# The first loop of a hybrid diffusion layer: shift rows on TensorE beside the scale rows, four row buffers ahead, and the context's x loaded last

## The chip, the cores and the metric

One NeuronCore of a Trainium2 chip runs the whole kernel. The metric is the device time of one execution in microseconds (us); lower is better. The kernel before was timed three times: 1124.28, 1126.04 and 1126.17 us, median 1126.04.

## What is computed

One layer over 512 latent tokens and 256 context tokens of width 1024: a half-step SwiGLU FFN, token mixing (latent attention beside a chunked gating MLP), and a second half-step FFN. Each sublayer first normalizes and modulates its input:

```python
def rms_norm(x, w):
    xf = x.astype(jnp.float32)
    y = xf * lax.rsqrt(jnp.mean(xf * xf, axis=-1, keepdims=True) + EPS)
    return (y * w.astype(jnp.float32)).astype(x.dtype)

def modulate(h, shift, scale):
    return h * (1 + scale) + shift

def ffn_sublayer(h_in, shift, scale, gate, norm_w, w1, w3, w2):
    h = modulate(rms_norm(h_in, norm_w), shift, scale)
    return h_in + 0.5 * gate * swiglu(h, w1, w3, w2)
...
    mx = jnp.split((jax.nn.silu(c) @ w_ada + b_ada)[:, None, :], N_MOD, axis=-1)
    mc = jnp.split((jax.nn.silu(c_ctx) @ w_ada + b_ada)[None, None, :], N_MOD, axis=-1)
...
    x = ffn_sublayer(x, mx[0], mx[1], mx[2], norm1_w, ffn1_w1, ffn1_w3, ffn1_w2)
    ctx = ffn_sublayer(ctx, mc[0], mc[1], mc[2], norm1_w, ffn1_w1, ffn1_w3, ffn1_w2)
```

`mx` and `mc` are the nine modulation vectors of the latent and of the context tokens. The first FFN needs two of them before anything else can be multiplied: the scale (`mx[1]`, `mc[1]`) and the shift (`mx[0]`, `mc[0]`), each a product of a 1024-vector with a 1024 x 1024 part of `w_ada`.

## The kernel before

All activations lie transposed: the 1024 features in eight slices `k` of 128 partitions, the tokens along the free axis, as two groups of 256 latent and 128 context tokens. Each fp32 matrix product is made of three fp32r products: an operand is split into a rounded high part and a remainder, and high x high, high x low and low x high are summed in PSUM.

The **first loop** goes over the eight slices of features. For slice `k` it makes the slice's shift and scale, makes the modulated activations of that slice, and multiplies them with the slice's part of the first four up-projection tiles (`NFIRST = 2` pairs). What one step consists of, with the names of the profile:

- loads on SyncE's queue (SP): `scale` (512 KB, the scale's columns of `w_ada` for this slice), `shift` (512 KB), and `raw` (256 KB of FFN weights). `x` comes first; the context's part of `x` comes in two loads of 128x8x128 (`load_x(..., slice(256, 384))`).
- the scale by TensorE: `ada_row` (L330 to 333) makes a row of four partial sums with eight matmuls of 32 weight columns, each in one of four 32-partition quarters of the bank `pa`; ScalarE copies it to `row`; `ada_col` (L340 to 342) turns it into a column pair (latent, context) with one matmul by `sel`; ScalarE makes `a` of it.
- the shift by VectorE: `ada_sum` calls `ada_dot` (L296), a multiply of the 128x1024 `shift` tile with `cb`, silu(c) spread over all partitions, that sums along the row into `accs` (the product itself goes to `junk`). There is one for the latent and one for the context vector of each slice, 16 in all. ScalarE adds the bias (`ada_s`, output `s`).
- `first_x` (VectorE) makes `hfull` = x * a * rstd; `first_h` (ScalarE) adds the shift and rounds to `hh`; `first_l` (VectorE) makes the remainder `hl`. `oph` (ScalarE) and `opl` (VectorE) split the weights.
- `first_half` and `first_mm` (L596, L604): the latent matmuls into `big`. `first_ctx` (L589): 12 matmuls for the context's part of one slice into two `mm` banks.
- once: the squares of `x`, their sum over features by a matmul with `ones` (L470, `sums`), the root `r` and the steps for `v` = rstd; for the context these are `square1`, `ctx_add`, and `sumc`, in the middle of the loop.

A list scheduler normally orders the program, but the first loop is under `nc.ordered = True`: VectorE, ScalarE and GpSimd keep the order in which the code is written, and so do the matmuls and the SP loads, which are wrapped in `pin`. These instructions all appear under line L59, the wrapper, so they are told apart by their tiles. A load waits until its buffer is free and until the load issued eight before it has landed, and all later loads wait behind it.

After the loop the first FFN goes on in the same manner, with weight tiles `raw` and `block` (from `wst`); its own modulation products (`ada_rest`) still use `cb` and `ada_dot`.

Of the kernel before, what the change touches and what calls it, by code (L numbers as in the profile page):

```python
# [17 lines left out]
P = 128  # L18
# [20 lines left out]
OPS = 5  # L39
# [134 lines left out]
def layer_kernel(ctx: ExitStack, tc: tile.TileContext, xT, wfirst, wst, wada, wuq, wkpe, cols, wrope, vnw, rope, out):  # L174
# [39 lines left out]
    accs = const.tile([P, NK, 2], F32, name="accs")  # L214
# [46 lines left out]
    sblk, units, raws_ = [], [], []  # L261

    def first_scale(k):
        ra = sp.tile([P, D], F32, tag="sa", bufs=3, name=f"scale_{k}")
        pin(nc.sync.dma_start(ra, wada[k][:, :D]))
        units.append([ra])

    def first_shift(k):
        if k % 2 == 0:
            pool, tag, bufs = (sp, "sb", 1) if k == 4 else (st.raw_pool, "block", BLOCKS)  # L270
            sblk.append(pool.tile([P, 2048], F32, tag=tag, bufs=bufs, name=f"shift_{k}"))
        rs_ = sblk[-1][:, (k % 2) * D : (k % 2) * D + D]
        pin(nc.sync.dma_start(rs_, wada[k][:, D:]))
        units[k].append(rs_)
# [6 lines left out]
    def first_units(k):  # L281
        first_scale(k)
        first_shift(k)
        first_raw(k)

    for k in range(3):
        first_units(k)
    nc.vector.tensor_reduce(sel, ident.rearrange("p (q c) -> p c q", c=32)[:, 0:2, :], axis=AX.X, op=ALU.add)
# [7 lines left out]
    def ada_dot(raw, c, which, to=None):  # L296
# [3 lines left out]
        nc.vector.scalar_tensor_tensor(  # L300
            out, raw, 1.0, cb[:, which, :], ALU.mult, ALU.mult,
            accum_out=acc[which][:, c : c + 1] if to is None else to,
        )
# [26 lines left out]
    def ada_row(d):  # L330
        for kt in range(NK):
            q = slice(kt % 4 * 32, kt % 4 * 32 + 32)
            pin(nc.tensor.matmul(pa[q, :P], scw[:, kt, :], units[d][0][:, kt * P : kt * P + P], start=kt < 4, stop=kt >= NK - 4))
# [6 lines left out]
    def ada_col(row, d):  # L340
        o = pcol[:, 2 * d : 2 * d + 2]
        pin(nc.tensor.matmul(o, row, sel, start=True, stop=True))
# [9 lines left out]
    def ada_shift(d, which):  # L352
        ada_sum(d, which)
        ada_s(d, which)
# [108 lines left out]
    def square1(j):  # L463
        sq = sp.tile([P, 512], F32, tag="sqx0", bufs=4, name=f"sq0_1{j}")
# [7 lines left out]
    def rstd_tiles(which):  # L472
        n = parts[which][1]
        return [sp.tile([P, n], F32, bufs=1, name=f"{s}{which}") for s in ("r0", "v")]
# [52 lines left out]
    put_cb(0)  # L527
    nc.vector.tensor_scalar_add(b1, col[:, COL_B : COL_B + 72], 1.0)
# [3 lines left out]
    def oph(k):  # L532
        ops[k] = st.pair() if k != OPS else [sp.tile([P, 512], F32R, tag="sqx0", bufs=4, name=f"op5{p}") for p in "hl"]
# [20 lines left out]
    put_cb(1)  # L554
    oph(0)
    steps(0)
    ada_row(0)
    row = ada_copy(0)
    late_sums(1)
    ada_col(row, 0)  # L560
    ada_sum(0, 0)
    ada_s(0, 0)
    root(1)
# [3 lines left out]
    first_units(3)  # L567
    ada_row(1)
    row = ada_copy(1)
    first_l(0, 0, 0)  # L570
    oph(1)
    steps(1)
    first_x(0, 0, 1)
    opl(1)
    first_h(0, 0, 1)
    first_units(4)
    load_x(0, 4, slice(256, 384))
# [35 lines left out]
    def step_open(k):  # L613
        ada_col(row, k + 1)
        if k + 2 < NK:
            ada_row(k + 2)

    sqs = []
    first_half(0)
    ada_col(row, 1)  # L620
    first_l(0, 0, 1)
    ada_row(2)
    row = ada_copy(2)
    ada_sum(1, 0)
    ada_s(1, 0)
    first_half(1)
    first_x(1, 0)
    first_h(1, 0)
    ada_sum(2, 0)
    first_l(1, 0)  # L630
    oph(2)
    opl(2)
    ada_s(2, 0)
    first_scale(5)
    load_x(4, 4, slice(256, 384))
    first_shift(5)
    first_raw(5)

    step_open(1)
    first_x(2, 0)  # L640
    first_h(2, 0)
    row = ada_copy(3)
    ada_sum(0, 1)
    first_l(2, 0)
    ada_sum(3, 0)
    oph(3)
    opl(3)
    ada_s(3, 0)
    ada_s(0, 1)
    step_mm(1)  # L650

    step_open(2)
    first_x(3, 0)
    first_h(3, 0)
    row = ada_copy(4)
    ada_sum(1, 1)
    oph(4)
    for j in (0, 1):
        sqs.append(square1(j))
    first_l(3, 0)  # L660
    ada_sum(4, 0)
    opl(4)
    ada_s(1, 1)
    ada_s(4, 0)
    step_mm(2)
    for k in (6, 7):
        first_scale(k)
        first_raw(k)
    for k in (6, 7):
        first_shift(k)  # L670

    step_open(3)
    first_x(4, 0)
    first_h(4, 0)
    for j in (2, 3):
        sqs.append(square1(j))
    row = ada_copy(5)
    ada_sum(5, 0)
    first_l(4, 0)
    ctx_add(2, 0)  # L680
    ctx_add(3, 1)
    ada_s(5, 0)
    oph(5)
    opl(5)
    ctx_add(2, 3)
    nc.vector.tensor_add(sqs[2][:, 0:256], sqs[2][:, 0:256], sqs[2][:, 256:512])
    step_mm(3)

    step_open(4)
    first_mm(4, 0)  # L690
    sumc = mm()
    sums(sumc, sqs[2][:, 0:256], True, True)
    first_mm(4, 1)
    first_x(5, 0)
    first_h(5, 0)
    row = ada_copy(6)
    first_l(5, 0)
    ada_sum(6, 0)
    ada_s(6, 0)
    rc = rstd_tiles(1)  # L700
# [4 lines left out]
    for j in (0, 1):  # L705
        first_x(j, 1)
        first_h(j, 1)
    ada_sum(2, 1)
    for j in (0, 1):
        first_l(j, 1)  # L710

    pcs += [mm() for _ in range(NFIRST)]
    step_open(5)
    first_x(6, 0)
    first_h(6, 0)
    row = ada_copy(7)
    ada_sum(3, 1)
    for j in (2, 3):
        ada_s(j, 1)
    first_l(6, 0)  # L720
    for j in (2, 3):
        first_x(j, 1)
        first_h(j, 1)
    ada_sum(7, 0)
    for j in (2, 3):
        first_l(j, 1)
    step_mm(5)
    for j in (0, 1):
        first_ctx(j)
    ada_s(7, 0)  # L730
    oph(6)
    opl(6)

    step_open(6)
    first_x(7, 0)
    first_h(7, 0)
    ada_sum(4, 1)
    first_l(7, 0)
    for j in (2, 3):
        first_ctx(j)  # L740
    oph(7)
    opl(7)
    ada_sum(5, 1)
    for j in (4, 5):
        ada_s(j, 1)
        first_x(j, 1)
        first_h(j, 1)
    ada_sum(6, 1)
    for j in (4, 5):
        first_l(j, 1)  # L750
    ada_sum(7, 1)
    for j in (6, 7):
        ada_s(j, 1)
        first_x(j, 1)
        first_h(j, 1)
    for j in (6, 7):
        first_l(j, 1)
    step_mm(6)

    step_mm(7)  # L760
    for j in range(4, NK):
# [1477 lines left out]
```

## Time and profile before

| | |
|---|---|
| median of three runs | 1126.04 us |
| the profiled execution | 1126.13 us |
| its span, first to last instruction | 1124.3 us |
| TensorE busy | 1109.6 us (99%) |
| VectorE busy | 906.1 us (81%) |
| ScalarE busy | 540.1 us (48%) |
| GpSimd busy | 311.4 us (28%) |
| first matmul after the first loop | at 66.94 us |

The span is counted from the first instruction; all positions below are us from there. The execution's own time is 1.8 us longer than its span. PE is TensorE, DVE VectorE, ACT ScalarE, SPq the queue of SyncE that issues loads. A row of the timeline reads: start, length, engine, line, operation, output <- inputs, number of instructions, and in brackets the idle time of the engine before it with what ended it. An fp32 matmul that isn't fp32r is recorded as two (x16 for eight). Lengths of neighbours on one engine overlap, so that the time an instruction takes in a stream is the distance between starts.

### The profile page before, as it was taken

The page shows a single profiled execution, that of the slowest core. Times are in us where ns is not written, and L with a number is a line of the kernel's source. Part 1 is how long each engine was busy: PE and PEld are TensorE (multiplying, and loading weights), DVE is VectorE, ACT ScalarE, POOL GpSimd, SP SyncE. Part 2 cuts the span into 40 slices and gives each one's busy share as a digit, 9 for nine tenths or more (in the row PEclk, how much of TensorE's full clock was granted, in tenths as well). Part 3 has the DMA queues.
Part 4 walks back from the last instruction along what each step waited for, and adds up shares of the span by engine and source line. Part 5 has one row for each costly group of instructions (what it writes and reads, how often), then busy time and mean ns, then how long its engine had stood idle before and what let it go on. Part 6 is the DMA issues. An engine that isn't in the chain of part 4 may idle for free.

```text
span 1124.3 us, 18769 instructions
## 1 busy us (share of the span) xinstructions
PE 1109.6 (99%) x7078; PEld 1060.7 (94%) x7078; DVE 906.1 (81%) x1669; ACT 540.1 (48%) x1119; POOL 311.4 (28%) x268
## 2 busy tenths in 40 slices
PE   8799999999999999999999999999999999999998
PEld 6699999999999999999998889999989989898997
DVE  7989999888888778866855899978886969686884
ACT  5555422441344213444755559985553535353451
POOL 0002402420343013300008427750014425162330
PEclk9999999999999999999999999999999999999999
DMA  9630253244234664322233211003221422233302
GB/s 350 215 113 20 102 194 121 96 164 151 94 131 150 230 207 167 129 66 87 85 131 93 76 38 35 25 20 116 73 95 57 148 79 84 105 113 113 114 1 94
DMA packets 35674, 125.89 MB, mean 112 GB/s; under 512 B 3712, under 2 KB 10624, under 8 KB 30976
## 3 DMA queue, kind: packets, MB, share of 16 engines
q1 hardware_dynamic: 35440, 124.63, 32.8%
q8 instruction: 56, 0.92, 0.3%
q14 instruction: 34, 0.28, 0.1%
q10 hardware_dynamic: 144, 0.06, 0.0%
HBM read 122.58 MB, written 2.10 MB: 111 GB/s over the span
## 4 chain that ended last, share of the span: by engine, by line
PE 91%; DVE 6%; ACT 1%; issue 1%; DMA 0%; POOL 0%; SPq 0%; DVEq 0%; POOLq 0%; ACTq 0%
PE mm L59 57%; PE one L59 20%; PE big L59 8%; PE mm L168 2%; PE mm L169 2%; PE mm L170 2%; DVE junk L59 1%; PE mm L589 1%; DVE opl L59 1%; DVE hfB L59 1%; DVE hfull L59 1%; DVE hl L59 1%; PE big L604 1%; DMA x<-xT 0%; DVE v L59 0%
## 5 line engine op out<-in xcount | busy, mean ns | idle before, releaser
L59 DVE TENSOR_TENSOR opl<-block,oph 128x512 fp32r<-128x512 f32 x216 | 192.3, 897 | 29.7 <-ACT oph L59 26.9
L59 POOL TENSOR_TENSOR block<-block 128x512 f32<-128x512 f32 x69 | 104.9, 1521 | 391.1 <-DVE opl L59 388.4
L59 ACT CAST oph<-block 128x512 fp32r<-128x512 f32 x216 | 133.8, 621 | 111.9 <-PE mm L59 85.1
L59 PE MATMUL mm<-gh,oph 128*128 128x384 f32 (+1 forms) x440 | 155.4, 353 | 0.0
L59 PE MATMUL mm<-gh,opl 128*128 128x384 f32 (+1 forms) x440 | 155.0, 352 | 0.0
L59 PE MATMUL mm<-gl,oph 128*128 128x384 f32 (+1 forms) x440 | 154.9, 352 | 0.0
L59 DVE SCALAR_TENSOR_TENSOR x<-mm,g,x 128x256 f32<-128x256 f32 (+2 forms) x184 | 84.6, 498 | 48.5 <-PE mm L59 48.2
L59 ACT CAST oph<-raw 128x512 fp32r<-128x512 f32 x115 | 69.9, 620 | 78.6 <-PE mm L59 53.1
L59 PEld LDWEIGHTS mm<-gh,opl 128*128 128x128 f32 x440 | 82.6, 188 | 5.7
L59 PEld LDWEIGHTS mm<-gl,oph 128*128 128x128 f32 x440 | 82.6, 188 | 5.6
L59 PEld LDWEIGHTS mm<-gh,oph 128*128 128x128 f32 x440 | 82.6, 188 | 5.6
L59 POOL TENSOR_TENSOR block<-s,block 128x512 f32<-128x512 f32 x35 | 48.0, 1371 | 143.7 <-DVE opl L59 143.1
L59 DVE TENSOR_TENSOR opl<-raw,oph 128x512 fp32r<-128x512 f32 x115 | 77.4, 688 | 7.2 <-ACT oph L59 6.5
L59 PE MATMUL mm<-hh,oph 128*128 128x384 f32 x192 | 64.9, 338 | 0.0
L59 PE MATMUL mm<-hh,opl 128*128 128x384 f32 x192 | 64.5, 336 | 0.0
L59 PE MATMUL mm<-hl,oph 128*128 128x384 f32 x192 | 64.5, 336 | 0.0
L59 DVE SCALAR_TENSOR_TENSOR junk<-raw,cb 128x1024 bf16<-128x1024 f32 x48 | 62.2, 1309 | 0.3 <-DMA raw<-wada 0.3
L59 POOL TENSOR_TENSOR s<-block 128x512 f32<-128x512 f32 x34 | 55.6, 1634 | 9.9 <-DMA block<-wst 9.9
L59 PE MATMUL one<-hh,opl 128*128 128x384 f32 x144 | 48.4, 336 | 0.0
L59 PE MATMUL one<-hh,oph 128*128 128x384 f32 x144 | 48.4, 336 | 0.0
L59 PE MATMUL one<-hl,oph 128*128 128x384 f32 x144 | 48.4, 336 | 0.0
L59 DVE SCALAR_TENSOR_TENSOR raw<-raw,cb 128x1024 f32<-128x1024 f32 x32 | 41.0, 1289 | 8.1 <-DMA raw<-wada 8.1
(685 smaller groups left out, 3403.0 us busy)
## 6 DMA issues: line engine op xcount, KB each, us to landing
raw<-wst SPq DMA_DIRECT2D x77, 512.0 KB, 3.9
block<-wst SPq DMA_DIRECT2D x36, 1024.0 KB, 4.9
raw<-wada SPq DMA_DIRECT2D x56, 512.0 KB, 4.3
scale<-wada SPq DMA_DIRECT2D x8, 512.0 KB, 8.4
shift<-wada SPq DMA_DIRECT2D x8, 512.0 KB, 8.9
x<-xT SPq DMA_DIRECT2D x5, 512.0 KB, 6.3
raw<-wfirst SPq DMA_DIRECT2D x8, 256.0 KB, 7.6
out<-x SPq DMA_DIRECT2D x7, 256.0 KB, 2.2
```

The lines of the kernel that those rows point to most:

```text
L59: return lambda *a, **k: self.tc.keep_in_program_order(f(*a, **k))
L168: nc.tensor.matmul(out, lh, rh, start=first, stop=False, skip_group_check=more)
L169: nc.tensor.matmul(out, lh, rl, start=False, stop=False, skip_group_check=more)
L170: nc.tensor.matmul(out, ll, rh, start=False, stop=last, skip_group_check=more)
L589: pin(nc.tensor.matmul(o, l[:, c], r, start=k == 0 and m == 0 and w == 0, stop=k == NK - 1 and m == 2, skip_group_check=True))
L604: pin(nc.tensor.matmul(two(pbs[i]), l[:, c], lat(r, k), start=False, stop=k == NK - 1 and m == 2, skip_group_check=True))
```

## The change

The shift is made like the scale. The shift's weights are laid out as the scale's are, and `ada_row` now makes 16 matmuls into the same bank: eight for the scale, with silu(c) in columns 0 and 1 of the 32 weight columns, and eight for the shift, with silu(c) in columns 2 and 3 (the tile `scw` is 34 wide, and the two halves are windows into it). `sel` has four columns, `ada_col` gives four, and ScalarE makes both `a` and `s` from them. The 16 `ada_dot` of the loop, `accs` and `ada_s` are gone.

```diff
-    scw = sp.tile([P, NK, 32], F32, bufs=1, name="sc")
-    sc = scw[:, :, 0:2]
-    sel = sp.tile([P, 2], F32, bufs=1, name="sel")
+    scw = sp.tile([P, NK, 34], F32, bufs=1, name="sc")
+    sc = scw[:, :, 2:4]
+    sel = sp.tile([P, 4], F32, bufs=1, name="sel")
...
+    def first_rows(k):
+        pool, tag, bufs = (sp, "sa", 2) if k % 2 else (st.raw_pool, "block", BLOCKS)
+        t = pool.tile([P, 2048], F32, tag=tag, bufs=bufs, name=f"scale_{k}")
+        units.append((t[:, :D], t[:, D:]))
+        for w in range(2):
+            pin(nc.sync.dma_start(units[k][w], wada[k][:, w * D : w * D + D]))
...
     def ada_row(d):
-        for kt in range(NK):
-            q = slice(kt % 4 * 32, kt % 4 * 32 + 32)
-            pin(nc.tensor.matmul(pa[q, :P], scw[:, kt, :], units[d][0][:, kt * P : kt * P + P], start=kt < 4, stop=kt >= NK - 4))
+        for w in range(2):
+            for kt in range(NK):
+                q = slice(kt % 4 * 32, kt % 4 * 32 + 32)
+                pin(nc.tensor.matmul(pa[q, :P], scw[:, kt, 2 - 2 * w : 34 - 2 * w], units[d][w][:, kt * P : kt * P + P],
+                                     start=w == 0 and kt < 4, stop=w == 1 and kt >= NK - 4))
...
     def ada_col(row, d):
-        o = pcol[:, 2 * d : 2 * d + 2]
+        o = pcol[:, 4 * d : 4 * d + 4]
         pin(nc.tensor.matmul(o, row, sel, start=True, stop=True))
         nc.scalar.activation(
-            pairs[0][1][:, d, :], o, AF.Identity, bias=b1n[:, d : d + 1], scale=col[:, COL_N1 + d : COL_N1 + d + 1])
-
-    def ada_sum(d, which):
-        ada_dot(units[d][1], d, which, accs[:, d, which : which + 1])
-
-    def ada_s(d, which):
-        nc.scalar.activation(mod_s[0][which][:, d : d + 1], accs[:, d, which : which + 1], AF.Identity, bias=col[:, d : d + 1])
+            pairs[0][1][:, d, :], o[:, 0:2], AF.Identity, bias=b1n[:, d : d + 1], scale=col[:, COL_N1 + d : COL_N1 + d + 1])
+        nc.scalar.activation(pairs[0][0][:, d, :], o[:, 2:4], AF.Identity, bias=col[:, d : d + 1])
...
-    first = np.concatenate([t[:, :, 1].transpose(2, 1, 0, 3).reshape(NK, P, 1024), t[:, :, 0].transpose(2, 3, 0, 1).reshape(NK, P, 1024)], 2)
+    first = np.concatenate([t[:, :, 1].transpose(2, 1, 0, 3).reshape(NK, P, 1024), t[:, :, 0].transpose(2, 1, 0, 3).reshape(NK, P, 1024)], 2)
```

Everything else in the loop is written in another order. The loads of four slices are issued at once instead of three, the context's `x` is loaded after seven of the eight `raw` tiles, its squares come in step 5 instead of steps 2 and 3 and its sum in step 6 instead of step 4, and all eight `first_ctx` come after the last latent matmul. `put_cb(1)`, ScalarE's copy of the context's `cb`, moves ahead of the first root. The loop's later part now reads:

```python
    for k in range(2, 5):
        step_open(k)
        next_h(k + 1)
        row = ada_copy(k + 2)
        first_l(k + 1, 0)
        oph(k + 2)
        opl(k + 2)
        if k == 2:
            first_raw(7)
        step_mm(k)
```

VectorE in the middle of the loop, before. A row is line, operation, output <- inputs and shape; `junk` is the output of a shift product, the number after a tile's name (`shift_0`) the slice where it has one:

```order
L59 TENSOR_TENSOR opl_373_374<-raw_252_253,oph_371_372 128x512
L59 SCALAR_TENSOR_TENSOR hfull_114<-x_71,a0_79,v0_214 128x2x256
L59 SCALAR_TENSOR_TENSOR junk_405_406,accs_87<-shift_0_129,cb_107 128x1024
L59 SCALAR_TENSOR_TENSOR hl_103<-hfull_114,s0_78,hh_102 128x2x256
L59 SCALAR_TENSOR_TENSOR junk_418_419,accs_87<-shift_4_279,cb_107 128x1024
L59 TENSOR_TENSOR opl_410_411<-raw_281_282,oph_408_409 128x512
```

The same place now, and on to the squares of the context's `x`:

```order
L59 TENSOR_TENSOR op6l_521<-raw_406_407,op6h_520 128x512
L59 SCALAR_TENSOR_TENSOR hfull_113<-x_71,a0_79,v0_215 128x2x256
L59 SCALAR_TENSOR_TENSOR hl_102<-hfull_113,s0_78,hh_101 128x2x256
L59 TENSOR_TENSOR op7l_561<-raw_441_442,op7h_560 128x512
L59 TENSOR_TENSOR sq0_11_566<-sq0_11_566,sq0_10_564 128x512
L59 TENSOR_TENSOR sq0_12_568<-sq0_12_568,sq0_11_566 128x512
L59 TENSOR_TENSOR sq0_13_570<-sq0_13_570,sq0_12_568 128x512
L59 TENSOR_TENSOR sq0_13_570<-sq0_13_570 128x256
L59 SCALAR_TENSOR_TENSOR hfull_113<-x_71,a0_79,v0_215 128x2x256
```

The two products between the modulations of neighbouring slices are gone; the adds of the squares now stand behind the split of the last weight tile and ahead of slice 7's `hfull`.

SyncE's loads from slice 4 on, before (`scale_4` is slice 4's; 128x8x128 is the context's `x`, and the last rows' `raw` and `block` from `wst` are weights for after the loop):

```order
L265 DMA scale_4_277<-wada 128x1024
L273 DMA shift_4_279<-wada 128x1024
L278 DMA raw_281_282<-wfirst 128x512
L258 DMA x_71<-xT 128x8x128
L265 DMA scale_5_343<-wada 128x1024
L258 DMA x_71<-xT 128x8x128
L273 DMA shift_4_279<-wada 128x1024
L278 DMA raw_347_348<-wfirst 128x512
L265 DMA scale_6_436<-wada 128x1024
L278 DMA raw_438_439<-wfirst 128x512
L265 DMA scale_7_441<-wada 128x1024
L278 DMA raw_443_444<-wfirst 128x512
```

And now (one `scale` tile holds scale and shift, so x2 is both):

```order
L267 DMA scale_4_276<-wada 128x1024 x2
L267 DMA scale_5_279<-wada 128x1024 x2
L271 DMA raw_346_347<-wfirst 128x512
L267 DMA scale_6_349<-wada 128x1024 x2
L271 DMA raw_358_359<-wfirst 128x512
L267 DMA scale_7_396<-wada 128x1024 x2
L271 DMA raw_406_407<-wfirst 128x512
L257 DMA x_71<-xT 128x8x128 x2
L127 DMA block_785_786<-wst 128x2048
L271 DMA raw_441_442<-wfirst 128x512
```

The context's loads moved behind slice 6's `raw`; the last `raw`, slice 7's, now stands behind both of them and behind a 1024 KB `block`.

TensorE at a step of the loop, before and then now (`row` is the copy that `ada_col` reads, `mm_157_158` the bank of the rows):

```order
L342 MATMUL mm_159_160<-sel_119,row_5_465 128x2
L333 MATMUL mm_157_158<-scale_6_436,sc_118 32x128 x8
L604 MATMUL big_285_286<-hh_102,oph_408_409 128x512 x2
L604 MATMUL big_285_286<-hh_102,opl_410_411 128x512 x2
L604 MATMUL big_285_286<-hl_103,oph_408_409 128x512 x2
```

```order
L334 MATMUL mm_159_160<-sel_118,row_5_477 128x4
L324 MATMUL mm_157_158<-scale_6_349,sc_117 32x128 x16
L581 MATMUL big_282_283<-hh_101,oph_435_436 128x512 x2
L581 MATMUL big_282_283<-hh_101,opl_437_438 128x512 x2
L581 MATMUL big_282_283<-hl_102,oph_435_436 128x512 x2
```

The row takes 16 matmuls instead of eight. Behind the loop each engine has the same instructions in the same order as before.

More of the change, by code (lines that the diff above doesn't have):

```diff
@@ L279, in first_raw @@
         raws_.append(rw[:, :W1])
[L281 to L288, printed above, removed]
+    for k in range(4):
+        first_rows(k)
+        if k < 3:
+            first_raw(k)
+    nc.vector.tensor_reduce(sel, ident.rearrange("p (q c) -> p c q", c=32)[:, 0:4, :], axis=AX.X, op=ALU.add)
     warm = mm()
@@ L294, in layer_kernel, with ada_dot @@
     nc.scalar.activation(epsc2, sc[:, 0, 0:1], AF.Abs_reciprocal_sqrt, bias=epsc, scale=0.0)
[L296 removed]
+    def ada_dot(raw, c, which):
         out = raw
@@ L566, in layer_kernel @@
     opl(0)
-    first_units(3)
-    ada_row(1)
+    root(1)
     row = ada_copy(1)
     first_l(0, 0, 0)
[L571 to L577, printed above, removed]
+    first_raw(3)
+    first_rows(4)
+    first_rows(5)
     pbs = bigs(4)
@@ L677, in layer_kernel @@
[L677 to L690, printed above, removed]
-    sumc = mm()
[L692 to L700, printed above, removed]
+    first_raw(6)
@@ new lines, in layer_kernel @@
+    for k in (0, 4):
+        load_x(k, 4, slice(256, 384))
+    for k in range(2, 5):
[8 more added lines that the diff above has]
+        step_mm(k)
+    step_open(5)
+    next_h(6)
+    row = ada_copy(7)
+    first_l(6, 0)
+    oph(7)
+    opl(7)
+    for j in range(4):
+        sqs.append(square1(j))
+    for a, b in ((1, 0), (2, 1), (3, 2)):
+        ctx_add(a, b)
```

168 lines of the change are left out of this document (49 added, 119 removed).

## The prediction

> **What bounds the kernel now.** I cut the span into stretches and asked for the busy time of each engine (PE, then DVE after the weight loads PEld). The columns are stretch, its length, busy us of PE, PEld, DVE, ACT, POOL, the granted clock, the DMA engines' share and GB/s.
>
> ```profile
> 12.23:28.00 15.77, 13.05 (x136) 10.00 (x135) 14.88 (x28) 8.76 (x23) 0.00 (x0) 1.00 1.05 389
> 44.00:51.44 7.44, 3.85 (x28) 3.28 (x28) 7.44 (x16) 3.83 (x11) 0.00 (x0) 1.00 0.27 78
> 67.10:1124.30 1057.20, 1052.99 (x6673) 1014.32 (x6671) 850.17 (x1563) 503.43 (x1036) 310.68 (x262) 1.00 0.31 102
> ```
>
> From 67.10 on TensorE is busy for 1052.99 of 1057.20 us: that part is bound by matmuls, and a loop that ends earlier moves it forward whole. In the loop it is otherwise: from 44.00 to 51.44 VectorE has no idle time and TensorE works half the time. What VectorE does in a step, from the timeline (start, length), with the one group of the shift products over the loop:
>
> ```profile
> 32.71 0.75 DVE L59 SCALAR_TENSOR_TENSOR hfull<-x,a,v 128x512 f32<-128x512 f32 x1
> 33.38 1.22 DVE L59 SCALAR_TENSOR_TENSOR junk<-shift,cb 128x1024 bf16<-128x1024 f32 x1
> 34.52 0.75 DVE L59 SCALAR_TENSOR_TENSOR hl<-hfull,s,hh 128x512 fp32r<-128x512 f32 x1
> L59 DVE SCALAR_TENSOR_TENSOR junk<-shift,cb 128x1024 bf16<-128x1024 f32 x16 | 19.5, 1218 | 0.0
> ```
>
> A shift product holds VectorE for 1.14 us (33.38 to 34.52). Sixteen make 18.2 us, and they were never idle-waited for (the last column is 0.0): VectorE is the bound from about 14 to 51, and what it is late with keeps TensorE waiting.
>
> **What the change removes and adds.** It removes those 18.2 us from VectorE. It adds 16 - 8 = 8 matmuls per slice to TensorE. A step there:
>
> ```profile
> 26.51 0.73 PE L604 MATMUL big<-hh,oph 128*128 128x512 f32 x2
> 28.91 0.62 PE L604 MATMUL big<-hl,oph 128*128 128x512 f32 x2
> 30.11 0.38 PE L342 MATMUL mm<-sel,row 128*128 128x2 f32 x2 [0.57 <-ACT row L59]
> 30.43 0.65 PE L333 MATMUL mm<-scale,sc 128*32 128x128 f32 x16
> 31.00 0.72 PE L604 MATMUL big<-hh,oph 128*128 128x512 f32 x2
> ```
>
> The column takes 0.32 (30.11 to 30.43), a scale row 0.57, the twelve large matmuls 2.88 (five of six pairs in 28.91 - 26.51 = 2.40). A shift row has the same shapes, so I price it at 0.57 too: 4.6 us in eight slices. The wider column (128x4 for 128x2), and on ScalarE one activation of a column pair in place of two of a column, go at nothing: ScalarE idles in each step, and the most that two more columns can cost is a second column, 0.32 x 8 = 2.6 us. A step becomes 0.32 + 1.14 + 2.88 = 4.34 us on TensorE; VectorE now needs three instructions for it, about 0.7 each, so **TensorE becomes the bound of the steps**.
>
> The copy of the second `cb`, now ahead of the first root on ScalarE, falls into idle time:
>
> ```profile
> 12.34 0.47 ACT L59 ACTIVATE r<-mm,epsc 128x256 f32<-128x256 f32 x1 [1.28 <-PE mm L470]
> 12.71 1.00 ACT L59 COPY cb<-big 128x1024 f32<-128x1024 f32 x1
> ```
>
> ScalarE waits 1.28 us ahead of the root, and the copy takes 1.00; I take nothing for it; 1.0 is the most, if `big` comes only when the root's bank does.
>
> Order of events:
>
> ```profile
> 12.23 0.65 PE L333 MATMUL mm<-scale,sc 128*32 128x128 f32 x16
> 12.80 1.13 PE L470 MATMUL mm<-sq,ones 128*128 128x256 f32 x4
> 16.47 0.74 PE L596 MATMUL big<-hh,oph 128*128 128x256 f32 x4 [1.06 <-ACT hh L59]
> 18.04 0.28 PE L342 MATMUL mm<-sel,row 128*128 128x2 f32 x2
> ```
>
> Row 0 starts at 12.23, as before. From there to the column of step 2 TensorE has 4 rows (4.56), 3 columns (0.96), two late sums (about 0.6 of the 1.13 shown, as starts go), two first halves (16.47 to 18.04, 1.57 each) and a step's matmuls (2.88): 12.1 us, so 24.3 without a wait. Waits remain, since the first two halves hang on copies, activations and `hh` in turn: they are between nothing and the 2.72 us that the first stretch above leaves (15.77 - 13.05). I take 1.8, nearer to before's, since only the shift products drop out of that chain: step 2 at 26.1. Steps 2 to 5 bring it to 43.5, if the rows' loads are there.
>
> **The loads.** DMA is what the change moves most:
>
> ```profile
> 0.00:20.00 20.00, 16.24 (x125) 13.19 (x126) 12.09 (x29) 12.39 (x25) 0.69 (x6) 1.00 0.94 340
> 10.00:24.00 14.00, 11.35 (x121) 9.00 (x121) 12.11 (x27) 8.07 (x20) 0.00 (x0) 1.00 1.03 404
> 24.00:30.00 6.00, 5.48 (x37) 3.79 (x35) 5.82 (x9) 2.93 (x9) 0.00 (x0) 1.00 1.12 340
> 13.31 0.43 SPq L273 DMA_DIRECT2D shift<-wada  x1
> shift<-wada SPq DMA_DIRECT2D x1, 512.0 KB, 9.7
> 20.24 3.10 SPq L265 DMA_DIRECT2D scale<-wada  x1
> ```
>
> The DMA engines are full (share 1.03) at 404 GB/s, and give 340 while the context's `x` comes (24 to 30). The slice-3 shift, issued at 13.31, lands 9.7 us later at 23.0. Up to it 7.2 MB are ordered, and 340 x 20 us = 6.80 MB are moved by 20.0, so its bytes are through at 21.0: a landing lies 2.0 behind its bytes. In the new order slice 4's pair ends at 8.5 MB (moved at 24.2, lands at 26.2; row 4 asks for the shift at 27.0) and each later pair comes 1.3 MB or 3.3 us on, under the 4.34 of a step: slice 7's lands at about 35, and row 7 starts at 39.4. The rows are fed.
>
> The **last weight tile** isn't. Ahead of slice 7's `raw` now stand the context's `x` (1.05 MB) and a `block` (1.05 MB); with it 14.8 MB are ordered. From 8.4 MB at 24.0, 6.4 MB at 404 GB/s take 15.8 us, 0.9 more for the context's slower packets (6 us at 340 instead of 404), 2.0 to land: **42.7**. The instruction behind a context load also sits 3.10 us in SP's queue (20.24): two in a row, from 29.8, bring the issue of that `raw` to about 36, which leaves it 6.7 us, so the bytes decide.
>
> Behind that wait on ScalarE stand its split (0.6), all four squares, and slice 7's `a`, `s` and `hh`; on VectorE `opl`, the adds, `hfull` and `hl`. On TensorE the sum of squares stands ahead of half of step 6. The prices of this chain, all as they ran before:
>
> ```profile
> 30.48 1.15 ACT L59 ACTIVATE sq<-x 128x512 f32<-128x512 f32 x2
> 37.17 0.68 DVE L59 TENSOR_TENSOR sq<-sq,sq 128x512 f32<-128x512 f32 x1
> 37.89 0.43 DVE L59 TENSOR_TENSOR sq<-sq 128x256 f32<-128x256 f32 x1
> 38.23 0.74 DVE L59 SCALAR_TENSOR_TENSOR hfull<-x,a,v 128x512 f32<-128x512 f32 x1
> 38.37 0.70 PE L470 MATMUL mm<-sq,ones 128*128 128x256 f32 x2 [0.37 <-DVE sq L59]
> 39.01 0.72 ACT L59 ACTIVATE hh<-hfull,s 128x512 fp32r<-128x512 f32 x1 [2.24 <-DVE hfull L59]
> 42.38 0.42 DVE L59 SCALAR_TENSOR_TENSOR v<-mm,r 128x256 f32<-128x256 f32 x1 [0.72 <-ACT r L59]
> 43.76 0.88 DVE L59 SCALAR_TENSOR_TENSOR hfull<-x,a,v 128x256 f32<-128x256 f32 x2
> ```
>
> 42.7 + 0.6 + 2.2 (four squares, two pairs that overlap a little) = 45.5; add 0.7 and fold 0.4: the sum's matmul at 46.6. TensorE has come to it at 43.5 + 0.32 + 1.44 = 45.2 and **waits 1.4 us**. It then has 0.35 + 1.44 + 2.88 of latent work, to 51.3. Meanwhile VectorE: `hfull` 0.7, `hh` on ScalarE 0.7, `hl` 0.7 (48.7), the steps of `v` 1.4 (42.38 to 43.76; 50.1), two context `hfull` 0.9 and `hl` 0.5: 51.6. So TensorE starts the context's matmuls as soon as it is free, and the second one at 51.6. Their pace before, the first matmul behind the loop, and VectorE's last instruction in it:
>
> ```profile
> 64.11 0.28 PE L589 MATMUL mm<-hh,oph 128*128 128x256 f32 x1
> 66.82 0.28 PE L589 MATMUL mm<-hh,opl 128*128 128x256 f32 x1
> 66.94 0.34 PE L59 MATMUL mm<-hh,oph 128*128 128x384 f32 x1
> 62.41 0.49 DVE L59 SCALAR_TENSOR_TENSOR hl<-hfull,s,hh 128x256 fp32r<-128x256 f32 x1 [0.24 <-ACT hh L59]
> ```
>
> 23 in 2.71 us is 0.118 each, and 95 end at **62.8**; VectorE's 1.9 us for a pair of slices stays ahead of TensorE's 2.8. The next weights are ready: VectorE is done with the loop at about 57, where before its last `hl` (62.41) ended at 62.9. Their splits do meet a new wait, as they take the operand buffers of slices 0 to 4, which the context's matmuls now free one after the other from 53 to 58.5; that is still ahead of 62.8. The next matmul starts at 62.8 instead of 66.94: **4.1 us earlier**. Against the profiled execution (1126.13, 1.8 more than its span, and 0.1 from the median) that is 1122.0.
>
> **A rule against the trace.** Part of the 4.1 is clock:
>
> ```profile
> 32.10:35.51 3.41, 1.98 (x10) 1.30 (x8) 3.41 (x7) 2.55 (x7) 0.00 (x0) 1.00 1.04 400
> 49.16:52.57 3.41, 1.59 (x12) 1.32 (x11) 3.33 (x8) 1.97 (x5) 0.00 (x0) 1.00 0.90 300
> 52.57:55.98 3.41, 3.41 (x18) 3.31 (x17) 3.41 (x6) 1.44 (x3) 0.00 (x0) 0.51 0.48 160
> ```
>
> The granted clock halves for the 3.41 us from 52.57, which costs 1.7. The stretch ahead of it was 1.59 busy of 3.41 (47%); 32.10 to 35.51 with 1.98 (58%) had no such sequel. So I expect a halving behind a stretch that is under about half busy, and none after the change, where a 1.4 us wait leaves 2.0 of 3.41. It is close enough to be a rival. The Trainium skill, page "TensorE: Matmul & The Clock Gate", section "HAM oscillation — how this bites in real kernels", asks only that no idle gap be longer than about 3.4 us. By that rule neither kernel would lose clock, and the sum would stay at 4.1 without this rival; the trace disagrees, since no single gap in 49.16:52.57 can be over 1.82 us (3.41 - 1.59).
>
> **The rivals.**
> - *TensorE's own work ends the loop.* If the last tile or the adds come earlier than I have it, the waits at 45.2 go: 43.5 + 0.32 + 2.88 + 0.35 + 2.88 + 96 x 0.118 = 61.2, or 59.4 without the early 1.8 as well: 1120.4 to 1118.6. For: 2.0 us of landing lag is read from one load. Against: the bytes are counted, and ScalarE goes in order.
> - *The clock halves again*, behind the wait at 45.2 or that of the first halves: 1.7 lost, 1123.7.
> - *The loads set the pace.* At 340 GB/s from 24.0 on, 6.4 MB take 18.8 us, the last tile lands at 44.8, and all behind it is 2.1 later: 1124.1, within what can't be told from no change (0.2%, 2.3 us). For: context and `block` now run one after the other. Against: full share and 404 with plain rows.
> - *Slower: the shift's matmuls wait for the scale's in their common bank.* If each of the four quarters must first finish the scale's last matmul (0.273 us alone, the row below), a row costs 4 x 0.273 = 1.1 more, 8.7 us in all: 61.2 + 8.7 = 69.9, 3.0 later than now, 1129.1. It makes the kernel slower by 0.2% from 1.0 us per row on ((66.94 + 2.3 - 61.2) / 8). Against: within a scale row the second four matmuls already follow the first four into the same quarters, and all eight take 0.57.
>
> ```profile
> L333 PE MATMUL mm<-scale,sc x128: 272/273/297, 12.2 to 40.9; 128*32 128x128 f32 x128
> ```
>
> **How the numbers follow.** My forecast, 1122.0, has 0.50; TensorE's own work 0.15; the clock 0.15; the loads 0.13; the bank 0.07. The range reaches from the lowest bound, 1118.6, over the loads' 1124.1 with a little for a mix of clock and loads, to 1124.6. Faster by over 0.2% means under 1123.8: the forecast, TensorE's own work and just over half of the clock's case, 0.74. Slower is the bank's 0.07, the rest 0.19.
>
> **What would show it.** Right: a row of 16 matmuls takes about 1.14 us, with no wait for loads from row 3 on; steps 2 to 5 are 4.3 apart; ScalarE waits for slice 7's `raw` until about 42.7; TensorE waits once, some 1.4 us, at its sum of squares; the loop ends near 62.8; the clock stays whole. Wrong: TensorE waiting for `scale` loads at rows 4 to 7, idle VectorE time that doesn't turn into TensorE time, or a gain of the loop's end that is gone by 1124.

## The result, and the profile after

The changed kernel took **1131.91 us** in the median of four runs (1131.01 to 1133.80), the kernel before, run four times beside it, 1125.84 us (1124.28 to 1126.17). The ratio is 1.0063 with a 95% interval of 1.0051 to 1.0075: **slower by 0.6%**, where the prediction had 1122.0 us and a range up to 1124.6. The profiled execution of the changed kernel took 1131.4 us, with a span of 1129.6. The kernel before, timed 40 more times beside the runs below, takes either 1123.9 to 1125.0 us (22 times) or 1125.6 to 1126.1 (18 times), and its profiled execution, at 1126.13, belongs to the longer ones.

The split of the span at the first matmul behind the loop says where the time is. First the busy times of the changed kernel in the two stretches that the prediction showed of before, and from its first matmul behind the loop to its end (columns as there):

```profile
12.23:28.00 15.77, 14.43 (x212) 11.88 (x212) 10.40 (x19) 8.65 (x24) 0.00 (x0) 1.00 1.03 406
44.00:51.44 7.44, 4.35 (x20) 3.49 (x19) 5.88 (x12) 4.59 (x10) 0.00 (x0) 1.00 0.53 210
63.76:1129.60 1065.84, 1062.23 (x6674) 1023.49 (x6672) 849.32 (x1561) 501.54 (x1033) 308.49 (x262) 1.00 0.30 101
```

The same last stretch of the kernel before, from its own first matmul behind the loop:

```profile
66.94:1124.30 1057.36, 1053.15 (x6674) 1014.48 (x6672) 850.33 (x1563) 503.59 (x1036) 310.68 (x262) 1.00 0.31 102
```

The loop ends at 63.76 instead of 66.94, 3.18 us earlier; VectorE is no longer full in it (10.40 of 15.77 where it was 14.88). All that is lost is lost **behind** the loop: 1065.84 us instead of 1057.36, 8.48 more, with the same 6674 matmul records, the same clock of 1.00, and TensorE busy throughout. The chain of work that ended last shows how (start, length, engine, line, count), before:

```profile
142.02 45.78 PE mm L59 x264
187.81 8.32 PE one L59 x48
202.36 8.32 PE mm L59 x48
856.18 5.66 PE one L59 x48
```

and after:

```profile
139.95 45.83 PE mm L59 x264
185.78 8.45 PE one L59 x48
200.56 8.45 PE mm L59 x48
858.30 5.76 PE one L59 x48
```

The pieces of 48 are up-projections of the first FFN (8.32 us; 384 columns) and of the second (5.66 us; 256 columns). They became 1.6% and 1.8% longer, each by the same amount every time. The pieces of 264 are down-projections, and they did not change (45.78 and 45.83). The groups of one shape, first of before, then of after (busy us, mean ns of one):

```profile
L59 PE MATMUL mm<-gh,oph 128*128 128x384 f32 x296 | 99.2, 335 | 0.0
L59 PE MATMUL one<-hh,opl 128*128 128x384 f32 x144 | 48.4, 336 | 0.0
L59 PE MATMUL one<-t2h,opl 128*128 128x256 f32 x36 | 10.0, 279 | 0.0
```

```profile
L59 PE MATMUL mm<-gh,oph 128*128 128x384 f32 x296 | 99.2, 335 | 0.0
L59 PE MATMUL one<-hh,opl 128*128 128x384 f32 x144 | 48.7, 338 | 0.0
L59 PE MATMUL one<-t2h,opl 128*128 128x256 f32 x36 | 10.3, 285 | 0.0
```

Nothing waits (0.0 in the last column), and the same product with moving tile `gh` keeps its 335 ns. In the program as it is laid out, one thing differs between these products. Tiles are allocated from both ends of SBUF, the on-chip memory; a matmul reads two operands there, the weights (loaded by the records of PEld) and the moving tile. The weights `oph` and `opl`, `gh` and `gl` stand at the lower end, behind the pool of constants; `hh`, `hl`, `u2` to `u4`, `t1` to `t4` and `b11` to `b22` without `b12`, the moving tiles of the up-projections, at the upper end. Deleting `accs` took 64 bytes per partition out of the constants, and so moved the lower end: the first `oph` from byte 56736 to 56672 of a partition, while `hh` stayed at 180192. Here and below, a distance is what is left of it when multiples of 256 bytes are taken away: 180192 - 56736 is 482 times 256 and 64, 180192 - 56672 is 482 times 256 and 128. So the moving tile of an up-projection stood 64 bytes above the weights before and stands 128 above them now; in the down-projections both moved, and the distance stays 0. Summed over the starts in both traces, the matmuls with weights `oph` or `opl` and a moving tile at the upper end took 4.62 us longer at 384 columns (1752 matmuls) and 3.10 at 256 (1728), together 7.7 of the 8.48; those with `b12h` and `b12l`, whose moving tiles alone of `b11` to `b22` stand at the lower end, took 0.04 less (48 matmuls). That the pace follows this distance was the theory; the rivals were that the new loop itself slows what follows, and that the weights' own address counts.

### The profile page after: what moved, and what is told of

Its sections match the earlier page's. It is cut to its first block, busy times and chain, and to the rows that moved or that the text cites. A ratio compares the mean times of both kernels' runs of the same rounds, so it can differ in the third digit from the quotient of the medians.

```text
span 1129.6 us, 18985 instructions
## 1 busy us (share of the span) xinstructions
PE 1119.8 (99%) x7206; PEld 1071.9 (95%) x7206; DVE 889.5 (79%) x1637; ACT 537.8 (48%) x1111; POOL 309.2 (27%) x268
## 4 chain that ended last, share of the span: by engine, by line
PE 95%; DMA 2%; ACT 1%; DVE 1%; issue 0%; POOL 0%; SPq 0%; DVEq 0%; POOLq 0%; ACTq 0%
PE mm L59 56%; PE one L59 20%; PE big L59 8%; PE mm L168 2%; PE mm L169 2%; PE mm L170 2%; PE mm L566 1%; PE big L581 1%; DMA scale<-wada 1%; PE big L170 1%; PE big L168 1%; PE big L169 1%; DMA raw<-wfirst 1%; PE mm L324 1%; DMA x<-xT 0%
```

## The experiments

### The 64 bytes, put back, taken away, and balanced

Three edits. In the changed kernel, an unused tile where `accs` stood:

```diff
+    pad = const.tile([P, 16], F32, name="pad")
     epsc = const.tile([P, 1], F32, name="epsc")
```

> The changed kernel, with one unused tile of 64 bytes per partition in the pool of constants, where the dots' accumulator (accs) stood before the change. No instruction is added. Theory A (layout): the change lost time only because the removed tile moved the op tiles, which are TensorE's weights in the up-projections, 64 bytes down in SBUF, while the moving tiles hh and hl at the other end stayed. With the 64 bytes back, 48 matmuls of FFN1's up-projection take 8.32 us again (8.45 in the changed kernel) and the whole is some 9.5 us shorter: the loop's gain of 3.7 us stays and the time is about 1122. Theory B (the loop itself, or the runtime, has slowed the later matmuls): 8.45 us per 48 stays, and the time stays at 1131.9.

In the kernel before, `accs` taken from the loop's own pool at the upper end:

```diff
-    accs = const.tile([P, NK, 2], F32, name="accs")
...
+    accs = sp.tile([P, NK, 2], F32, bufs=1, name="accs")
```

> The kernel before the change, with its accumulator of 64 bytes per partition taken from the first loop's own pool at the other end of SBUF instead of the pool of constants. The loop is the old one, instruction for instruction. Theory A (layout): the weights move 64 bytes down as in the changed kernel, 48 matmuls of FFN1's up-projection take 8.45 us instead of 8.32, and the time is 1125.8 + 9.5 = about 1135. Theory B (the new loop slows what follows): 8.32 us and 1126.

In the changed kernel, 64 unused bytes at the upper end:

```diff
+    with right():
+        rpool = ctx.enter_context(tc.tile_pool(name="rpool", bufs=1))
+    rpad = rpool.tile([P, 16], F32, name="rpad")
```

> The changed kernel with 64 unused bytes per partition at the upper end of SBUF for the whole program, so that the moving tiles (hh, hl, u2 to u4, t1 to t4, b11 to b22) go down by 64 bytes like the weights did. Theory A1 (what counts is the distance between the moving tile and the weights): the distance is that of the kernel before again, 48 matmuls take 8.32 us, about 1122. Theory A2 (what counts is the address of the weights alone): 8.45 us and 1131.9. Theory B: 8.45 us and 1131.9 as well.

Measured: 1124.11 us with the bytes back (10 runs, 1122.74 to 1125.52; ratio to before 0.9993, 0.9984 to 1.0003), 1132.73 for the kernel before without them, 1124.21 with them at the upper end (one execution each). One piece of the chain each, in that order:

```profile
185.54 8.32 PE one L59 x48
```

```profile
187.43 8.45 PE one L59 x48
```

```profile
185.59 8.32 PE one L59 x48
```

All three agree with the distance, and both rivals fall: the old loop has the longer pace when only `accs` is moved, and the new loop has the shorter one with the weights still at their new address, once the moving tiles go down as well. One more rival is that the moving tiles meet not the weights but what other engines and the DMA read and write at the lower end, which moved along with the constants. The traces speak against it. Sorted by what else was at work, the starts of the up-projections' matmuls of 384 columns lie 176.0 ns apart in the changed kernel with VectorE busy and 175.9 with VectorE idle, 176.0 with a DMA under way and 176.0 without; in the kernel before it is 173.4, 173.4, 173.4 and 173.3. The pace hangs on the layout and not on what works beside TensorE.

The loop and the rest now separate cleanly (the rest is the span less the first matmul behind the loop):

| kernel | loop ends | rest |
|---|---|---|
| before | 66.94 | 1057.36 |
| after | 63.76 | 1065.84 |
| after, 64 bytes back | 64.67 | 1057.53 |
| before, `accs` at the upper end | 65.42 | 1065.58 |
| after, 64 bytes at the upper end | 64.75 | 1057.65 |

(The kernel before without its 64 bytes came out 2 us under the 1135 expected: its clock was halved from 16.4 to 19.8 us and from 36.9 to 40.3, not among the context's matmuls, its loop ended 1.5 earlier, and its rest grew by 8.2, where 9.5 were expected.) The 64 bytes are worth 7.8 us of the median (1131.91 to 1124.11). What they leave of the change is 0.7 us against the runs of before beside it (1124.81), not the 3.7 us expected. Against the profiled execution of before the loop still ends 2.3 earlier (64.67 and 66.94), but that execution is one of the longer ones. Part of what is missing is clock. Of the kernel with the bytes back, the wait in front of the sums of squares, and the stretch of halved clock behind it:

```profile
47.31 0.67 PE L454 MATMUL mm<-sq,ones 128*128 128x256 f32 x2 [3.56 <-DVE sq L59]
48.80:52.20 3.40, 3.40 (x10) 2.71 (x9) 3.12 (x8) 2.60 (x5) 0.00 (x0) 0.52 0.00 1
```

From that matmul to the first of the context's it needs 53.55 - 47.31 = 6.24 us, the changed kernel, without a halving in its profile, 51.93 - 47.32 = 4.61: the halving costs 1.6. To the end of the loop it is 64.67 - 47.31 = 17.36 against 63.76 - 47.32 = 16.44, as the context's matmuls regain 0.7. Nine of the ten runs have a mean clock of 0.997 or 0.998; the one at 1.000 is the fastest, 1122.74.

### How the pace depends on the distance

The unused tile with 8, 32, 64 and 24 in place of 16 columns (32, 128, 256 and 96 bytes), on top of the kernel with the squares first, which is the next experiment and took 1120.93 with 64 bytes. Each of the four ran once here. A larger tile moves the weights up and makes the distance smaller: it is 128 less the bytes.

> The kernel with the squares first, and its unused tile of 32 bytes in place of 64. The moving tile stands 128 - 32 = 96 bytes above the weights, counted in steps of 256 (64 with the 64 bytes: 8.32 us per 48 matmuls; 128 without: 8.45). If only a distance of exactly 128 is slow: 8.32 and about 1121. If the slowness grows with nearness to 128: between, 8.36 to 8.43 and 1123 to 1128. If the whole range from 96 on is slow: 8.45 and about 1129.5.

> The same with 128 unused bytes: distance 0, as in the down-projections, which ran at 0.1734 us per matmul in both kernels. If the distance is all that counts: 8.32 us per 48 in the up-projections, and 1121. If each stage has its own speed whatever the distance: not 8.32.

> The same with 256 unused bytes: distance -128, which is 128 again if what counts repeats every 256 bytes (8.45 us per 48, about 1129.5), and 384 if it repeats every 512 bytes or more (then 8.32 and 1121, unless that distance is slow too).

> The kernel with the squares first, with 96 unused bytes in place of 64: the moving tile stands 32 bytes above the weights (counted in steps of 256). So far: 64 is fast in both FFNs' up-projections (8.32 us per 48 matmuls of 384 columns; 280 ns for one of 256 columns), 0 is fast for 384 columns and slow for 256 (283 ns), 96 and 128 are slow for both. If 32 lies with 64: about 1120.9. If it lies with 0: about 1123.5. If each 32-byte offset is slow, as 96 is: 1130.

Measured, with the lengths of a piece of 48 in the two FFNs' up-projections:

| unused bytes | distance | us | first FFN | second FFN | rest |
|---|---|---|---|---|---|
| 32 | 96 | 1131.13 | 8.48 | 5.76 | 1067.60 |
| 64 | 64 | 1120.93 (5 runs) | 8.32 | 5.66 | 1057.54 |
| 96 | 32 | 1120.06 | 8.32, for a while 8.48 | 5.60 | 1056.85 |
| 128 | 0 | 1123.71 | 8.32 | 5.76 | 1060.45 |
| 256 | -128 | 1129.56 | 8.45 | 5.76 | 1065.85 |

A distance of -128 has the pace and the rest of 128, as an effect that repeats every 256 bytes would have it; this one pair is all that shows the repeat. It isn't one bad place at 128: 96 is slower still, and 0 is short for 384 columns and long for 256. With 96 bytes the pace changed within one execution, at the same addresses. From its timeline:

```profile
107.20 0.33 PE L59 MATMUL mm<-u4h,oph 128*128 128x384 f32 x1
...
109.11 0.34 PE L59 MATMUL mm<-u4h,opl 128*128 128x384 f32 x1
109.29 0.36 PE L59 MATMUL mm<-hh,oph 128*128 128x384 f32 x1
109.48 0.34 PE L59 MATMUL mm<-hl,oph 128*128 128x384 f32 x1
...
111.60 0.34 PE L59 MATMUL one<-hl,oph 128*128 128x384 f32 x1
```

From 107.20 to 109.11 eleven starts take 1.91 us, 0.174 each; one matmul is 0.02 longer, and from there on twelve take 2.12 us (109.48 to 111.60), 0.177 each, until the down-projection at 137. So the distance doesn't fix the pace alone: at 32 bytes two paces exist. Later sections come back to this.

### TensorE's wait in front of the sums of squares

The changed kernel's largest wait left in the loop (3.1 us; predicted 1.4). Two repairs, each on the kernel with the 64 bytes back, then both. The squares ahead of slice 7's casts:

```diff
-    oph(7)
-    opl(7)
     for j in range(4):
         sqs.append(square1(j))
...
     nc.vector.tensor_add(sqs[3][:, 0:256], sqs[3][:, 0:256], sqs[3][:, 256:512])
+    oph(7)
+    opl(7)
```

> The kernel with the 64 bytes back, and in the loop's sixth step the squares of the context and their sums stand ahead of the two casts of slice 7, which wait for slice 7's raw till 42.7 us. Theory A: TensorE's wait of 3.1 us in front of the matmuls of the sums of squares shrinks to some 0.8, the first stage ends at about 60.8 instead of 63.2, and the time is about 1120 (2 below the kernel with the 64 bytes alone). Rival: the wait moves to slice 7's casts or to the context's normalisation, and the time is that of the kernel with the 64 bytes alone, about 1122.

Slice 7's `raw` ordered ahead of the context's loads:

```diff
     first_raw(6)
+    first_raw(7)
     for k in (0, 4):
         load_x(k, 4, slice(256, 384))
...
-        if k == 2:
-            first_raw(7)
```

> The kernel with the 64 bytes back, its squares where the change put them (behind slice 7's casts), and slice 7's raw ordered on SP's queue ahead of the context's two loads and the last block, instead of behind them. Theory: that the raw lands only at 42.7 is what makes TensorE wait for the sums; it now lands some 2 MB earlier (by about 36), the context's loads 0.26 MB or 0.7 us later. ScalarE's wait goes, the squares start at about 40.5, TensorE's wait shrinks from 3.6 to under 1, no halved clock follows, and the time is about 1121. Rival: the context's x becomes the late one, or the loads on SP stall behind the raw's buffer, and the wait stays over 2 us: 1122.5 to 1124.

> The kernel with the 64 bytes back, and both repairs of the wait in front of the sums of squares: slice 7's raw ordered ahead of the context's loads, and the squares ahead of slice 7's casts. Each alone gave 1120.9 to 1121.0 with 0.55 and 1.25 us of that wait left. If the wait is all that is left of it: it goes, the first stage ends 0.5 us earlier (at about 61.2), about 1120.4. Rival: the context's x, now the last load, makes the squares late, and it stays at 1121.

Measured: 1120.93 (5 runs; ratio 0.9966, 0.9953 to 0.9979), 1121.02 (6 runs; 0.9967, 0.9954 to 0.9979) and, with both, 1121.67 (5 runs; 0.9966, 0.9953 to 0.9980, the runs of before beside it having their median at 1125.75). The wait of each, in that order:

```profile
44.59 0.67 PE L454 MATMUL mm<-sq,ones 128*128 128x256 f32 x2 [0.55 <-DVE sq L59]
```

```profile
45.42 0.67 PE L454 MATMUL mm<-sq,ones 128*128 128x256 f32 x2 [1.25 <-DVE sq L59]
```

```profile
42.49 1.16 ACT L59 ACTIVATE sq<-x 128x512 f32<-128x512 f32 x2 [0.33 <-DMA x<-xT]
45.25 0.67 PE L454 MATMUL mm<-sq,ones 128*128 128x256 f32 x2 [0.87 <-DVE sq L59]
```

Either repair brings the loop's end to 61.56 and 61.55, 3.1 us ahead of the kernel with the bytes back, and the clock stays at 1.000 in every run of the first two. In the profiles of both, the rest is 1057.54 and 1057.55: the whole gain of the loop arrives at the end. Both together are no better (62.24), as the rival had it, but its reason is the smaller part. The context's second load is then the last one, and the squares wait 0.33 for it at 42.49; still, the wait in front of the sums is shorter than with the second repair alone (0.87 and 1.25). The time is lost behind it: the second of the context's matmuls starts at 50.86 instead of 50.44, and those of the context's first slices follow each other every 0.118 us (15 starts from 51.20 to 52.97) instead of every 0.113 (15 from 50.77 to 52.47), with the same 64 bytes in place. The 0.113 also stands in the kernel with the bytes back, the 0.118 also in the one with the squares first, so at a distance of 64 there are two paces as well, in these matmuls; why, no run here tells.

### The shift products back on VectorE

The changed kernel with its buffers, loads and order, `accs` back in its place, eight matmuls per row, and two products on VectorE for each slice: the latent one in `ada_col`, the context's behind `opl`.

```diff
-        nc.scalar.activation(pairs[0][0][:, d, :], o[:, 2:4], AF.Identity, bias=col[:, d : d + 1])
+        ada_shift(d, 0)
...
         opl(k + 2)
+        ada_shift(k + 1, 1)
```

> The changed kernel's order, buffers and loads, but the shift products back on VectorE (two dots of 1.14 us for each slice, into the accumulator's 64 bytes, which restore the layout too) and no shift rows on TensorE. Theory (the products on VectorE bound the old loop): VectorE needs 3 x 0.7 + 2 x 1.14 = 4.4 us per step and 18 us in all, the steps of the loop come out 4.4 or more apart instead of 4.12, and the first stage ends 1 to 4 us later than with the rows on TensorE: 1124.5 to 1127. Rival: the landing of slice 7's raw at 42.7 ends the loop whichever engine makes the shift, and the dots fit beside it: the same 1124.1 as the kernel with the 64 bytes back.

Measured: 1134.50 (4 runs; ratio 1.0079, 1.0062 to 1.0095). The rest is 1057.39, so all of it is the loop, which ends at 76.11. One step of it (`scale` <- `scale`, `cb` is the context's product, `junk` the latent one):

```profile
30.86 0.53 PE L335 MATMUL mm<-sel,row 128*128 128x4 f32 x2 [2.83 <-ACT row L59]
31.96 1.22 DVE L59 SCALAR_TENSOR_TENSOR scale<-scale,cb 128x1024 f32<-128x1024 f32 x1
33.10 1.22 DVE L59 SCALAR_TENSOR_TENSOR junk<-scale,cb 128x1024 bf16<-128x1024 f32 x1
34.25 0.75 DVE L59 SCALAR_TENSOR_TENSOR hfull<-x,a,v 128x512 f32<-128x512 f32 x1
35.72 0.24 ACT L59 COPY row<-mm 128x128 f32<-128x128 f32 x1
36.12 0.29 PE L335 MATMUL mm<-sel,row 128*128 128x4 f32 x2
```

The steps are 5.26 apart (30.86 to 36.12; part of this one ran at half clock, but the step before it, 25.59 to 30.86, did not and is as long): both products stand between a column and `hfull`, and the next row's copy stands behind `hh` on ScalarE. The rival (the dots fit beside the last load) falls. But the loss is larger than the theory's, since this order wasn't made for them, and the halved clock comes in as well (17.1 us of the loop in all, from 17.3, 30.9 and 54.8 on). It shows that this order depends on having the shift on TensorE, and not what the shift alone is worth in an order of its own.

### The best version, and the pace once more

> The kernel with the squares first and 96 unused bytes (distance 32), timed. One look gave 1120.06, though its up-projection ran at 8.48 us per 48 matmuls from about 109 to 137 us, and at 8.32 before and after, with the same addresses. If that distance lets the slower pace come in by chance, as one matmul of 0.36 us at 109.29 suggests, the runs spread: between 1119.4 (never) and some 1128 (all the way). If it is a fixed stretch of the program, all runs lie within 0.5 of 1120. In either case faster than both kernels; the kernel with 64 bytes gave 1120.9.

> The kernel with the squares first and 32 unused bytes (distance 96) once more, in several runs. If that distance is slow by itself: all of them at about 1131. If its slow pace is one of two, entered by chance: some runs at 1121 to 1125.

Measured: 1119.72 for 96 bytes with the squares first (5 runs, 1119.71 to 1120.22; ratio to before 0.9957, 0.9944 to 0.9969), faster than the kernel before by 0.4% and, by the medians, than the changed one by 1.1%; and 1131.00 for 32 bytes (4 runs, 1130.90 to 1131.26). In this profile of the 96 bytes the excursion isn't there:

```profile
126.30 8.32 PE mm L59 x48
182.46 8.32 PE one L59 x48
851.36 5.60 PE one L59 x48
```

So at 32 bytes of distance the slower pace was there in one of the two profiled executions, for 28 us; at 96 bytes of distance all five executions were slow, and both profiles have 8.48 in every piece of the first FFN's up-projections. What happens between the reads of the moving tile and of the weights, and why one pace can give way to the other, no run here tells; it stays open.

## Why the prediction was wrong, point by point

**The step that failed** is the first one drawn from the profile: "that part is bound by matmuls, and a loop that ends earlier moves it forward whole". The first half held, and the second holds at a constant layout (rests of 1057.4 to 1057.7 at 64 bytes of distance, with loops that end anywhere from 61.55 to 76.11). It failed because the change also deletes a tile from the pool of constants, and behind the loop stand 1057 us of matmuls, of which the up-projections read one operand that hangs on that pool and one that doesn't. The description of the change listed `accs` as gone, and the prediction put no price on it. The sum was -4.1; the profiles have -3.2 for the loop and +8.5 for the rest. "Slower" had a chance of 0.07, for a different mechanism. Of the prediction's own signs of being wrong one came: a gain of the loop's end that is gone by the end of the kernel.

**The loop, term by term.** The columns and the rows of the changed kernel, from the timeline:

```profile
12.36 1.08 PE L324 MATMUL mm<-scale,sc 128*32 128x128 f32 x32
13.37 1.13 PE L453 MATMUL mm<-sq,ones 128*128 128x256 f32 x4
26.04 0.28 PE L334 MATMUL mm<-sel,row 128*128 128x4 f32 x2
30.15 0.28 PE L334 MATMUL mm<-sel,row 128*128 128x4 f32 x2
38.38 0.28 PE L334 MATMUL mm<-sel,row 128*128 128x4 f32 x2
42.46 0.28 PE L334 MATMUL mm<-sel,row 128*128 128x4 f32 x2
```

- A row of 16 takes 1.01 (12.36 to 13.37), predicted 1.14: right, and the rival that the common bank makes the shift wait for the scale is gone.
- The column of step 2 comes at 26.04 (26.1). That it is so close is in part luck: the waits ahead of it are 1.34 (15.77 - 14.43 in the first stretch above) where 1.8 was taken, and the work is longer than the 12.1 by about as much. The steps are 4.12 apart (4.34), and the wider column takes 0.21 (26.04 to 26.25), no more than the 0.32 of the narrow one. TensorE is busy all through steps 2 to 5 and is the bound there, as said; no row waits for a load from row 3 on.
- The end of the loop's chain, on all engines:

```profile
42.73 0.62 ACT L59 CAST op7h<-raw 128x512 fp32r<-128x512 f32 x1 [1.92 <-DMA raw<-wfirst]
43.25 2.19 ACT L59 ACTIVATE sq<-x 128x512 f32<-128x512 f32 x4
44.43 2.28 DVE L59 TENSOR_TENSOR sq<-sq,sq 128x512 f32<-128x512 f32 x3 [0.36 <-ACT sq L59]
46.75 0.43 DVE L59 TENSOR_TENSOR sq<-sq 128x256 f32<-128x256 f32 x1
47.32 0.67 PE L453 MATMUL mm<-sq,ones 128*128 128x256 f32 x2 [3.09 <-DVE sq L59]
63.76 0.34 PE L59 MATMUL mm<-hh,oph 128*128 128x384 f32 x1
```

- Slice 7's `raw` lets ScalarE go at 42.73 (42.7), from the count of bytes. Right. The queue took 3.41 for the context's two loads and 3.35 for the `block` behind them, and the `raw` was issued at 36.27 (36).
- The sums were at 47.32 (46.6): only one of the three adds was counted behind the squares, and they run one behind the other, 2.28 in all. TensorE came 1.0 earlier (44.23 instead of 45.2), as its steps were shorter. So the wait was 3.09 instead of 1.4: mis-sized, and with it the end, 63.76 instead of 62.8.
- The clock stayed whole in the profiled execution, but two of the four runs have a mean of 0.998 and 0.997, and they are the two slower ones (1132.43 and 1133.80 against 1131.01 and 1131.40). With the 64 bytes back, nine of ten runs had it: the rival that had a chance of 0.15 is what this loop mostly does, and with the layout held the median of 1124.11 is near its 1123.7. The rival that TensorE's own work ends the loop, at 61.2, is what either repair of the wait comes to (61.56 and 61.55).

## What to carry to other kernels

A change that adds or deletes even a small tile moves the addresses of everything allocated behind it; when matmuls bound a kernel, compare the time of one and the same matmul piece (here 8.32 and 8.45 us per 48) before you read a gain or loss as the change's own. Test it by putting the bytes back, and if the pace moves, scan the padding: here 32 and 96 unused bytes gave kernels 11 us apart, 1131.00 and 1119.72. A loop's gain is then read at its own end, and the rest apart from it.

## What the runs showed of the hardware that was not expected

- **The pace of fp32r matmuls follows the distance between moving tile and weights in SBUF, counted modulo 256 bytes.** In the up-projections with 384 columns: 0.1733 us a matmul (8.32 / 48) at 0, 32 and 64 bytes, 0.1760 at 128, 0.1767 at 96, and for 28 us of one execution at 32. With 256 columns: 0.117 (5.60 / 48) at 32, 0.118 at 64, 0.120 at 0, 96 and 128. The page "SBUF — State Buffer" of the Trainium skill, section "Who interferes with whom", gives TensorE two independent read ports, one for the moving operand and one for the weights. If that were the whole of it, the distance should make no difference; these runs show one, of 8.5 us in 1066. That it is the two reads that meet is not shown.
- **The clock goes by stretches of 3.41 us, not by the length of a gap.** In the traces' record of the granted clock, the full clock ahead of the halving lasts 47.79 us in the kernel before, 44.37 with the 64 bytes back and 40.96 with them at the upper end, which is 14, 13 and 12 times 3.41, and each of the three halvings lasts 3.41. In the last such stretch ahead of it TensorE was busy for 1.59 us (in the kernel before, with no wait over 0.95), 1.36 and 0.30. The gap of 3.11 of the last of them fills one stretch; the changed kernel's gap of 3.09 lies across a boundary, 12 times 3.41 behind the start of its record, and leaves both stretches at least half busy. The rows, first of the kernel with 64 bytes at the upper end (its wait, the stretch ahead of the halving, a part of the halving), then of the changed kernel:

```profile
47.13 1.05 PE L456 MATMUL mm<-sq,ones 128*128 128x256 f32 x2 [3.11 <-DVE sq L59]
43.87:47.28 3.41, 0.30 (x2) 0.18 (x2) 2.81 (x6) 1.76 (x5) 0.00 (x0) 1.00 0.93 377
48.00:49.00 1.00, 1.00 (x4) 0.81 (x3) 0.51 (x1) 0.98 (x3) 0.00 (x0) 0.50 0.11 45
```

```profile
42.51:45.92 3.41, 1.72 (x9) 1.11 (x7) 2.08 (x3) 3.10 (x7) 0.00 (x0) 1.00 0.99 389
45.92:49.33 3.41, 2.01 (x9) 1.73 (x10) 2.42 (x4) 1.38 (x3) 0.00 (x0) 1.00 0.60 237
```

  So the prediction's "under about half busy" fits these four when it is counted in these stretches (and the three halvings of the kernel with the shift products on VectorE, behind 1.69, 0.58 and 1.58 us of 3.41), and where they fall decides whether the same gap costs clock. It is no sharp limit: the kernel before with `accs` at the upper end was halved behind 1.83 and 2.00 us of 3.41. The rule of the Trainium skill that the prediction weighed (page "TensorE: Matmul & The Clock Gate", section "HAM oscillation — how this bites in real kernels": no idle gap over about 3.4 us) agrees with the wait of 3.56 with the bytes back, and the one of 3.11 shows that a shorter gap isn't safe. Waits of 0.55 and 1.25 had no halving in any of 11 runs.
